# Row sums of absolute values: one Abs pass in place of two Relu passes, and the last tile fetched in five pieces

## Chip, cores, metric

One core of a Trainium2 chip. The time is the device time of one execution in microseconds; it lies about 1.8 us above the span of the profile, which is the window of the instructions in the trace.

DVE is VectorE, ACT is ScalarE, SPq is the sequencer of SyncE, which issues the DMAs, POOL is GpSimd. A semaphore is a counter by which one unit tells another that it is done. A "landing" is the moment at which a DMA's semaphore lets a waiting instruction go. A load is moved in packets, here one for each row, shared out over 16 DMA engines; each engine adds a small one of 4 bytes at the end of its part. So a load of 128 whole rows is 9 packets an engine: the profile before counts 1296 packets for its nine DMAs, 9 x 9 x 16.

## The reference

```python
batch, dim = 1024, 4096                     # x: float32
def reference(x, axis):                     # axis = -1
    return np.sum(np.abs(x), axis=axis).astype(np.float32)
```

16.8 MB are read, 4 KB are written, and there is next to no arithmetic: the input must come in, and nothing more.

## The kernel before

Partition p holds the rows 8p to 8p+7; tile t is the t-th of these rows in all partitions, 128 x 4096. All eight tiles have a buffer of their own, so all loads are issued at once. VectorE reduces 2560 columns of each tile with a built-in absolute value. ScalarE takes the other 1536 twice, as Relu(x) and Relu(-x), each with a running sum.

```python
d_act = (int(D * 0.6 / (0.96 + 0.6)) // 128) * 128      # 1536
d_dve = D - d_act                                        # 2560
for t in range(T):                                       # T = 8
    xt = xs.tile([P, D], f32, name="xt")
    nc.sync.dma_start(out=xt, in_=x_t[t])
    nc.vector.tensor_reduce(out=dve_acc[:, t : t + 1], in_=xt[:, :d_dve],
        axis=mybir.AxisListType.X, op=mybir.AluOpType.add, apply_absolute_value=True)
    nc.scalar.activation(out=scratch, in_=xt[:, d_dve:], func=Relu, scale=1.0,
        accum_out=pos_acc[:, t : t + 1])                 # (names shortened)
    nc.scalar.activation(out=scratch, in_=xt[:, d_dve:], func=Relu, scale=-1.0,
        accum_out=neg_acc[:, t : t + 1])
nc.vector.tensor_add(out=pos_acc, in0=pos_acc, in1=neg_acc)
nc.vector.tensor_add(out=dve_acc, in0=dve_acc, in1=pos_acc)
nc.sync.dma_start(out=out_pt, in_=dve_acc)
```

## Time and profile before

| | before |
|---|---|
| time, median of 16 runs | 49.93 us (49.83 to 50.10) |
| span of the profiled run | 48.1 us |
| first tile lands | 7.87 us |
| tile to tile | 4.89 us |
| last tile lands | 42.1 us |
| result issued | 45.80 us |
| from there to the end of the span | 2.26 us |

The lower rows are read from the timeline: the start of a VectorE reduce that waited for its load is the landing, give or take 0.02 us. Read them as a budget: what comes before the last landing is transfer, and what comes after it is tail. The loads themselves, in the profile's list of DMA issues (size of each, and median time from issue to landing):

```profile
xt<-in_x_dram SPq DMA_DIRECT2D x8, 2048.0 KB, 22.6
out_dram<-dve_acc SPq DMA_DIRECT2D x1, 4.0 KB, 1.4
```

Eight loads of 2 MB stand in one queue, so a load "takes" 22.6 us, nearly all of it waiting behind others. The small one of the result shows the bare latency, 1.4 us.

### The profile page before, as it was taken

To read this page: it belongs to the slowest core of one execution; us is meant where nothing else is said; L and a number is where in the kernel's file an instruction comes from. 1 tells how busy PE (TensorE), PEld (TensorE's weight loads), DVE (VectorE), ACT (ScalarE), POOL (GpSimd) and SP (SyncE) were. 2 spreads that over 40 slices of the span, in tenths; PEclk is the share of its full clock that TensorE was granted. 3 is DMA by queue.
4 is the path that set the end of the run, shared out by engine and by line. 5 is a ranking of instruction groups with operands and counts; after the bars stand their busy time and mean duration, and the time that the engine had idled before them with its cause. 6 is when DMAs were issued, how large, how long until landed. Compare 5 with 4: busy or idle time off the path is not lost.

```text
span 48.1 us, 106 instructions
## 1 busy us (share of the span) xinstructions
DVE 22.9 (48%) x10; ACT 26.5 (55%) x33; POOL 0.2 (0%) x4
## 2 busy tenths in 40 slices
DVE  0000004980399039902991199109920993099500
ACT  3600004991399329931994199509960996089700
POOL 1000000000000000000000000000000000000000
DMA  0969999999999999999999999999999899300000
GB/s 0 218 286 409 409 436 436 436 423 436 436 436 436 436 436 436 436 436 436 436 436 436 436 436 436 436 409 423 423 423 436 382 436 423 136 0 0 0 3 0
DMA packets 1296, 16.78 MB, mean 349 GB/s; under 512 B 272, under 2 KB 272, under 8 KB 272
## 3 DMA queue, kind: packets, MB, share of 16 engines
q1 hardware_dynamic: 1296, 16.78, 83.1%
HBM read 16.78 MB, written 0.00 MB: 349 GB/s over the span
## 4 chain that ended last, share of the span: by engine, by line
DMA 79%; SPq 7%; ACT 6%; issue 1%; DVE 1%; ACTq 0%
DMA xt<-in_x_dram 79%; SPq L45 7%; ACT scratch L55 3%; ACT scratch L62 3%; DVE pos_acc L71 0%; DVE dve_acc L72 0%; ACTq L104 0%; ACTq L55 0%
## 5 line engine op out<-in xcount | busy, mean ns | idle before, releaser
L47 DVE TENSOR_REDUCE dve_acc<-xt 128x1 f32<-128x2560 f32 x8 | 22.6, 2820 | 22.4 <-DMA xt<-in_x_dram 22.4
L55 ACT ACTIVATE scratch<-xt 128x1536 f32<-128x1536 f32 x8 | 11.9, 1483 | 17.9 <-DMA xt<-in_x_dram 17.9
L62 ACT ACTIVATE scratch<-xt 128x1536 f32<-128x1536 f32 x8 | 11.9, 1483 | 0.2
L55 ACT ACT_TABLE_LOAD x1 | 1.3, 1283 | 0.7 <-PEq L90 0.7
L62 ACT ACTIVATION_READ_ACCUMULATOR scratch<-xt 128x1 f32 x8 | 1.5, 186 | 0.0
L55 ACT ACTIVATION_READ_ACCUMULATOR scratch<-xt 128x1 f32 x8 | 1.5, 186 | 0.0
L71 DVE TENSOR_TENSOR pos_acc<-pos_acc,neg_acc 128x8 f32<-128x8 f32 x1 | 0.2, 168 | 0.5 <-ACT scratch L62 0.5
L72 DVE TENSOR_TENSOR dve_acc<-dve_acc,pos_acc 128x8 f32<-128x8 f32 x1 | 0.2, 169 | 0.0
L90 POOL MEMSET const-bfloat16-1.0<- 128x1 bf16 x1 | 0.1, 103 | 0.0
L90 POOL MEMSET const-uint8-127<- 128x1 uint8 x1 | 0.1, 103 | 0.0
L90 POOL MEMSET const-float32-1.0<- 128x1 f32 x1 | 0.1, 100 | 0.0
L90 POOL MEMSET const-float32-0.0<- 128x1 f32 x1 | 0.1, 99 | 0.2 <-issue 0.2
## 6 DMA issues: line engine op xcount, KB each, us to landing
xt<-in_x_dram SPq DMA_DIRECT2D x8, 2048.0 KB, 22.6
out_dram<-dve_acc SPq DMA_DIRECT2D x1, 4.0 KB, 1.4
```

The lines of the kernel that those rows point to most:

```text
L45: nc.sync.dma_start(out=xt, in_=x_t[t])
L47: nc.vector.tensor_reduce(out=dve_acc[:, t : t + 1], in_=xt[:, :d_dve], axis=mybir.AxisListType.X, op=mybir.AluOpType.add, apply_absolute_ ...
L55: nc.scalar.activation(out=scratch, in_=xt[:, d_dve:], func=mybir.ActivationFunctionType.Relu, scale=1.0, accum_out=pos_acc[:, t : t + 1],)
L62: nc.scalar.activation(out=scratch, in_=xt[:, d_dve:], func=mybir.ActivationFunctionType.Relu, scale=-1.0, accum_out=neg_acc[:, t : t + 1],)
L71: nc.vector.tensor_add(out=pos_acc, in0=pos_acc, in1=neg_acc)
L72: nc.vector.tensor_add(out=dve_acc, in0=dve_acc, in1=pos_acc)
L90: nc = _bacc.Bacc("TRN2", target_bir_lowering=False, num_devices=1)
```

## The change

The intent: shorten the work that is left when the last data has landed. ScalarE does one Abs pass in place of two Relu passes; the whole tiles are split 2048 to 2048; the last tile comes in five loads, each given to one engine; one reduce over a common accumulator (zeroed by GpSimd at the start) replaces the two adds. The diff, cut to its core (an unused option for TensorE, off in the file, is left out):

```diff
+LAST = ((1280, 1), (1280, 0), (768, 1), (384, 0), (384, 1))  # columns, 1 for VectorE
+    acc = small.tile([P, T, S], f32, name="acc")             # S = 5
+    nc.gpsimd.memset(acc, 0.0)
     for t in range(T):
-        xt = xs.tile([P, D], f32, name="xt")
-        nc.sync.dma_start(out=xt, in_=x_t[t])
-        nc.vector.tensor_reduce(... in_=xt[:, :d_dve] ...)
-        nc.scalar.activation(... func=Relu, scale=1.0 ...)
-        nc.scalar.activation(... func=Relu, scale=-1.0 ...)
+        if t < T - 1:
+            xw = whole.tile([P, D], f32, name="xw")
+            nc.sync.dma_start(out=xw, in_=x_t[t])
+            nc.vector.tensor_reduce(out=acc[:, t, 2:3], in_=xw[:, :2048], ...)
+            nc.scalar.activation(out=scratch, in_=xw[:, 2048:], func=Abs, accum_out=acc[:, t, 0:1])
+            continue
+        for lo, hi, eng in chunks:                           # the five pieces of LAST
+            xt = xs.tile([P, max_chunk], f32, name="xt")[:, :cols]
+            nc.sync.dma_start(out=xt, in_=x_t[t][:, lo:hi])
+            if eng == 0:
+                nc.scalar.activation(... in_=xt, func=Abs, accum_out=acc[:, t, si : si + 1])
+            else:
+                nc.vector.tensor_reduce(out=acc[:, t, si : si + 1], in_=xt, ...)
-        nc.vector.tensor_add(out=pos_acc, in0=pos_acc, in1=neg_acc)
-        nc.vector.tensor_add(out=dve_acc, in0=dve_acc, in1=pos_acc)
-    nc.sync.dma_start(out=out_pt, in_=dve_acc)
+    nc.vector.tensor_reduce(out=out_sb, in_=acc, axis=X, op=add)
+    nc.sync.dma_start(out=out_pt, in_=out_sb)
```

More of the change, by code (lines that the diff above doesn't have):

```diff
@@ L7 @@
 from concourse._compat import with_exitstack
+LAST = ((1280, 1), (1280, 0), (768, 1), (384, 0), (384, 1))
+PE_WARM = False
+LOAD_BUFS = 5
 @with_exitstack
@@ L26 @@
     f32 = mybir.dt.float32
-    d_act = (int(D * 0.6 / (0.96 + 0.6)) // 128) * 128
-    d_dve = D - d_act
+    chunks = []
+    lo = 0
+    for c, eng in LAST:
+        chunks.append((lo, lo + c, eng))
+        lo += c
+    assert lo == D
+    S = len(LAST)
     x_t = x.rearrange("(p t) d -> t p d", t=T)
     out_pt = out.rearrange("(p t) -> p t", t=T)
-    xs = ctx.enter_context(tc.tile_pool(name="xs", bufs=min(T, 8)))
-    acc = ctx.enter_context(tc.tile_pool(name="acc", bufs=1))
+    xs = ctx.enter_context(tc.tile_pool(name="xs", bufs=LOAD_BUFS))
+    whole = ctx.enter_context(tc.tile_pool(name="whole", bufs=T - 1))
     small = ctx.enter_context(tc.tile_pool(name="small", bufs=1))
-    dve_acc = acc.tile([P, T], f32, name="dve_acc")
-    pos_acc = acc.tile([P, T], f32, name="pos_acc")
-    neg_acc = acc.tile([P, T], f32, name="neg_acc")
-    scratch = small.tile([P, d_act], f32, name="scratch") if d_act else None
-    for t in range(T):
-        xt = xs.tile([P, D], f32, name="xt")
-        nc.sync.dma_start(out=xt, in_=x_t[t])
-        nc.vector.tensor_reduce(
-            out=dve_acc[:, t : t + 1],
-            in_=xt[:, :d_dve],
-            axis=mybir.AxisListType.X,
-            op=mybir.AluOpType.add,
-            apply_absolute_value=True,
-        )
-        if d_act:
-            nc.scalar.activation(
-                out=scratch,
-                in_=xt[:, d_dve:],
-                func=mybir.ActivationFunctionType.Relu,
-                scale=1.0,
-                accum_out=pos_acc[:, t : t + 1],
+    if PE_WARM:
+        psum = ctx.enter_context(tc.tile_pool(name="psum", bufs=2, space=bass.MemoryType.PSUM))
+        ones = small.tile([P, 1], f32, name="ones")
+        nc.vector.memset(ones, 1.0)
+    acc = small.tile([P, T, S], f32, name="acc")
+    scratch = small.tile([P, 2048], f32, name="scratch")
+    out_sb = small.tile([P, T], f32, name="out_sb")
+    nc.gpsimd.memset(acc, 0.0)
+    max_chunk = max(hi - lo for lo, hi, _ in chunks)
+    for t in range(T):
+        if t < T - 1:
+            xw = whole.tile([P, D], f32, name="xw")
+            nc.sync.dma_start(out=xw, in_=x_t[t])
+            nc.vector.tensor_reduce(
+                out=acc[:, t, 2:3],
+                in_=xw[:, :2048],
+                axis=mybir.AxisListType.X,
+                op=mybir.AluOpType.add,
+                apply_absolute_value=True,
             )
@@ L63 @@
                 out=scratch,
-                in_=xt[:, d_dve:],
-                func=mybir.ActivationFunctionType.Relu,
-                scale=-1.0,
-                accum_out=neg_acc[:, t : t + 1],
-            )
-    if d_act:
-        nc.vector.tensor_add(out=pos_acc, in0=pos_acc, in1=neg_acc)
-        nc.vector.tensor_add(out=dve_acc, in0=dve_acc, in1=pos_acc)
-    nc.sync.dma_start(out=out_pt, in_=dve_acc)
+                in_=xw[:, 2048:],
+                func=mybir.ActivationFunctionType.Abs,
+                accum_out=acc[:, t, 0:1],
+            )
+            continue
+        si = 0
+        for lo, hi, eng in chunks:
+            cols = hi - lo
+            xt = xs.tile([P, max_chunk], f32, name="xt")[:, :cols]
+            nc.sync.dma_start(out=xt, in_=x_t[t][:, lo:hi])
+            if eng == 0:
+                nc.scalar.activation(
+                    out=scratch[:, :cols],
+                    in_=xt,
+                    func=mybir.ActivationFunctionType.Abs,
+                    accum_out=acc[:, t, si : si + 1],
+                )
+                si += 1
+            else:
+                nc.vector.tensor_reduce(
+                    out=acc[:, t, si : si + 1],
+                    in_=xt,
+                    axis=mybir.AxisListType.X,
+                    op=mybir.AluOpType.add,
+                    apply_absolute_value=True,
+                )
+                si += 1
+                if PE_WARM:
+                    pe_out = psum.tile([1, 256], f32, name="pe_out")
+                    nc.tensor.matmul(
+                        pe_out, lhsT=ones, rhs=xt[:, :256], start=True, stop=True
+                    )
+        assert si == S
+    nc.vector.tensor_reduce(
+        out=out_sb, in_=acc, axis=mybir.AxisListType.X, op=mybir.AluOpType.add
+    )
+    if PE_WARM:
+        pe_out2 = psum.tile([T, T], f32, name="pe_out2")
+        nc.tensor.matmul(pe_out2, lhsT=out_sb, rhs=out_sb, start=True, stop=True)
+    nc.sync.dma_start(out=out_pt, in_=out_sb)
 _INS = ['x', 'axis']
```

## The prediction

> **What bounds the kernel now.** I read the page first: the 40 slices (part 2) with the chain that ended last (part 4), to see whether transfers or engines fill the middle; then the groups (part 5) for durations; then the timeline of the last microseconds, because a kernel that is bound by transfers can only be shortened at its two ends.
>
> ```profile
> DVE  0000004980399039902991199109920993099500
> ACT  3600004991399329931994199509960996089700
> DMA  0969999999999999999999999999999899300000
> GB/s 0 218 286 409 409 436 436 436 423 436 436 436 436 436 436 436 436 436 436 436 436 436 436 436 436 436 409 423 423 423 436 382 436 423 136 0 0 0 3 0
> ...
> DMA 79%; SPq 7%; ACT 6%; issue 1%; DVE 1%; ACTq 0%
> ```
>
> Each slice is 1.2 us. The transfers are full from the fourth slice to the 34th, and both engines fall idle once in every tile. 79% of the final chain is the load of x. After the 35th slice nothing is moved, but the engines work for three more slices and the result is written: that is the tail that can be shortened.
>
> ```profile
> L47 DVE TENSOR_REDUCE dve_acc<-xt 128x1 f32<-128x2560 f32 x8 | 22.6, 2820 | 22.4 <-DMA xt<-in_x_dram 22.4
> L55 ACT ACTIVATE scratch<-xt 128x1536 f32<-128x1536 f32 x8 | 11.9, 1483 | 17.9 <-DMA xt<-in_x_dram 17.9
> L62 ACT ACTIVATE scratch<-xt 128x1536 f32<-128x1536 f32 x8 | 11.9, 1483 | 0.2
> L55 ACT ACT_TABLE_LOAD x1 | 1.3, 1283 | 0.7 <-PEq L90 0.7
> L55 ACT ACTIVATION_READ_ACCUMULATOR scratch<-xt 128x1 f32 x8 | 1.5, 186 | 0.0
> L71 DVE TENSOR_TENSOR pos_acc<-pos_acc,neg_acc 128x8 f32<-128x8 f32 x1 | 0.2, 168 | 0.5 <-ACT scratch L62 0.5
> ```
>
> Both engines idle only for the load. The timeline, in which a row starts with its start and its length in us:
>
> ```profile
> 37.23 2.82 DVE L47 TENSOR_REDUCE dve_acc<-xt 128x1 f32<-128x2560 f32 x1 [2.07 <-DMA xt<-in_x_dram]
> ...
> 42.12 2.82 DVE L47 TENSOR_REDUCE dve_acc<-xt 128x1 f32<-128x2560 f32 x1 [2.07 <-DMA xt<-in_x_dram]
> 42.18 1.48 ACT L55 ACTIVATE scratch<-xt 128x1536 f32<-128x1536 f32 x1 [1.71 <-DMA xt<-in_x_dram]
> 43.57 0.19 ACT L55 ACTIVATION_READ_ACCUMULATOR scratch<-xt 128x1 f32 x1
> 43.79 1.48 ACT L62 ACTIVATE scratch<-xt 128x1536 f32<-128x1536 f32 x1
> 45.18 0.19 ACT L62 ACTIVATION_READ_ACCUMULATOR scratch<-xt 128x1 f32 x1
> 45.40 0.17 DVE L71 TENSOR_TENSOR pos_acc<-pos_acc,neg_acc 128x8 f32<-128x8 f32 x1 [0.46 <-ACT scratch L62]
> 45.60 0.17 DVE L72 TENSOR_TENSOR dve_acc<-dve_acc,pos_acc 128x8 f32<-128x8 f32 x1
> 45.80 0.35 SPq L73 DMA_DIRECT2D out_dram<-dve_acc  x1
> ```
>
> Tiles land 42.12 - 37.23 = 4.89 us apart (the other tiles the same, from 7.87 us on). In a tile DVE works 2.82 us and ACT about 3.2, so DVE waits 2.07 and ACT 1.71: the middle is bound by transfer alone. The last tile lands at about 42.10, and the result's DMA is issued at 45.80. These 3.7 us are one tile on ScalarE (two Relu passes, 3.2 us) and two small adds. From the issue to the end of the span, 48.1, are 2.3 us, and the timed 50.0 us are 1.9 above the span; the change touches neither.
>
> **What the Trainium skill says.** (1) "ScalarE: Activation LUTs", What ACT_TABLE_LOAD costs: an ACTIVATE with immediate scale and bias takes 186 ns + 0.833 ns per element, and a table load 1283 ns. At 1536 elements that is 1466 ns; the trace has 1483, and 1283 for the load, so it agrees. Its section Table sets says abs and relu are in every set, so no second load; the order of instructions of the changed kernel has one load too. (2) "VectorE: DVE Perf Modes", the perf-mode tier table: tensor_reduce runs in 1x mode alone. The errata section of the page has (N+151)/0.96 ns for an fp32 tensor_tensor; used for the reduce, an estimate, it gives 2824 ns at N = 2560, against 2820 in the trace, so I use it for all reduces. (3) "DMA: Bandwidth & Descriptors", Bandwidth: its rule is 1 MiB or more a DMA, and Why small descriptors are slow gives some 3 cycles of fixed cost a packet. The trace has only 16 KB rows and the 32-byte result, so it doesn't show rows of 1.5 to 5 KB. (4) "Perfetto Trace Analysis", DMA Optimizations: splitting DMAs may let work start sooner; that is the change's intent, and the trace before, unsplit, cannot show it.
>
> **The change part by part.**
>
> *First seven tiles: two Relu passes become one Abs pass, split 2048 to 2048.* ACT per tile: 203 + 0.833 x 2048 = 1.91 us (203 is what the measured 1483 leaves), and with the accumulator's read about 2.1, from 3.2. DVE: (2048+151)/0.96 = 2.29 us, from 2.82. Worth nothing: both end before the next tile, which comes 4.89 us later.
>
> *Table load.* In the new order the load waits for the first tile, as the first activation waits for GpSimd's memset besides. So ACT begins tile 0 at 7.87 + 1.28 + 0.1 = 9.25 and is done at about 11.35. Tile 1 lands at 12.75. Hidden, with 1.4 us to spare.
>
> *Issues.* The queue now has 12 loads; the last four wait for landings of tiles 0 to 3 in turn (at 7.9, 12.8, 17.6 and 22.5 us by the starts above). Their data is due only from 38.8 us, so no gap. The result's DMA waits for tile 4's landing besides, 27.4 us: long over.
>
> *Last tile in five pieces.* A tile of 4096 columns takes 4.89 us, so 1.194 ns a column. From tile 6 at 37.23:
> piece 0 (1280, DVE) lands at 38.76; piece 1 (1280, ACT) at 40.29; piece 2 (768, DVE) at 41.20; piece 3 (384, ACT) at 41.66; piece 4 (384, DVE) at 42.12, if the rows' size costs nothing.
> DVE: tile 6 until 37.23 + 2.29 = 39.52; piece 0 (1431/0.96 = 1.49) until 41.03; piece 2 (0.96) from 41.22 to 42.18; piece 4 (535/0.96 = 0.56) from 42.20 to 42.76.
> ACT: tile 6 until 39.4; piece 1 (203 + 1066 = 1.27, with the read 1.4) from 40.35 until 41.75; piece 3 (203 + 320 = 0.52, with the read 0.62) from 41.80 to 42.4. So ACT is done before DVE.
> Final reduce over 40 elements: (40+151)/0.96 = 0.20 us, from 42.79 to 42.99; the result is issued at about 43.02, against 45.80.
> The tail after the landing falls from 3.70 to about 0.90: 2.8 us saved. It takes the place of the two adds too (0.37 with their gap).
>
> *What the pieces cost the transfer.* Each of the 16 DMA engines gets 8 rows and a completion a piece: 45 packets in place of 9 for the last tile, 36 more. Per packet: the skill's 3 cycles would be some 3 to 4 ns at the 850 MHz that the page names for the fabric, 0.13 us in all (an estimate). An upper bound from the trace: in its packet records the result's 144 packets, 9 an engine, pass in 0.19 us, 21 ns each; 36 x 21 = 0.76 us if all that came on top. I take 0.2 us.
>
> Sum: 50.0 - 2.8 + 0.2 = 47.4; the DVE reduce of piece 2 ends close to piece 4's landing, and a landing later by 0.2 hides a little of DVE's wait, 0.05. Predicted 47.3 us (span about 45.4).
>
> **The rivals.**
> A. The small rows slow the transfer by more than I allow. For: the skill's rule of 1 MiB, and rows of 1.5 KB are a tenth of those measured. Against: there is no gap between today's loads (4.89 us a tile is 429 GB/s, against 436 in the best slices), the pieces queue behind one another on full engines, and they are an eighth of the data. At the upper bound 47.9; to undo the gain the last tile's 4.89 us would have to become 7.7.
> B. An engine becomes the end: DVE behind on its three pieces, or false waits between DVE and ACT, which now write one accumulator tile. For: DVE's slack at piece 2 is just 0.19 us. Against: in the order of instructions each piece waits only for its own DMA and its own engine. If DVE were 0.5 us late: 47.8.
> C. The gain is hidden, because the kernel is bound by transfers (79% of the chain), and halving ACT's work helps an engine that waits anyway: 50.0. True for seven tiles, but the tail lies after the last transfer, so nothing hides it.
> D. The late issues leave a bubble or the late table load delays a tile: each would cost up to 1 us. The slacks above (16 us and 1.4 us) speak against it.
>
> **Range and chances.** With no cost of the pieces it is 47.15; with A's bound or B 47.8 to 47.9. The runs before spread by 0.2. So 46.9 to 47.9. Faster by over 2% means below 49.0, which needs 1.7 us of surprise: 0.96 faster, 0.03 same, 0.01 slower.
>
> **What would show it.** In the profile after: tiles 0 to 6 land within 0.1 us of before; ACT's first activation begins near 9.25; DVE's last piece begins at 42.2 to 42.5 and takes 0.56; the final reduce waits for DVE and not ACT; the result is issued at about 43.2; and the tail from there is 2.3 us still. It is wrong if the last piece lands after 42.9 (A), if DVE starts the last piece well after its landing or waits for ACT (B), if the slices before the end show a dip in GB/s (D), or if the span falls and the timed runs don't.

## The result, and the profile after

| | before | after |
|---|---|---|
| time, median | 49.93 us (16 runs) | 47.59 us (10 runs, 47.48 to 48.13) |
| ratio | | 0.954 (0.952 to 0.956) |
| tile 6 lands | 37.23 us | 37.23 us |
| last landing | 42.1 us | 42.37 us |
| result issued | 45.80 us | 43.28 us |
| from there to the end | 2.26 us | 2.43 us |

A ratio is the mean time of one kernel's fast runs over that of the other's of the same rounds, so not quite the ratio of the medians quoted. The kernel was run once more among the experiments: 47.69 us, ratio 0.952.

The same views as before. First the slices of the page for the transfers (each now 1.14 us), and the shares of the final chain:

```profile
DMA  0969999899999999999999999999999799995000
GB/s 0 215 244 459 444 430 445 373 401 430 459 459 459 444 416 401 387 416 459 459 459 444 430 387 387 430 444 459 459 430 430 323 408 417 392 395 188 0 4 0
...
DMA 88%; SPq 3%; DVE 2%; issue 1%; DVEq 0%
```

The transfer's share of the chain is 88%, up from 79%. Only part of that is the shorter span: the 37.9 us of transfer in the chain before would be 83% of 45.7 us. The rest is the way in which the chain is followed: it enters the transfers at 2.10 us in place of 4.17, because the load of the last piece was issued only when tile 3 had landed. The swings of GB/s look worrying and mean little, as a slice holds only some 30 packets of 16 KB (430 GB/s for 1.14 us); the landings are sharper, and all seven whole tiles land within 0.1 us of before. The groups:

```profile
L61 DVE TENSOR_REDUCE acc<-xw 128x1 f32<-128x2048 f32 x7 | 16.0, 2286 | 23.5 <-DMA xw<-in_x_dram 23.5
L68 ACT ACTIVATE scratch<-xw 128x2048 f32<-128x2048 f32 x7 | 13.4, 1909 | 16.1 <-DMA xw<-in_x_dram 16.0
L68 ACT ACT_TABLE_LOAD x1 | 1.3, 1283 | 7.9 <-DMA xw<-in_x_dram 7.9
L105 DVE TENSOR_REDUCE out_sb<-acc 128x8 f32<-128x40 f32 x1 | 0.2, 195 | 0.1
```

Each engine works less per tile and waits more for loads. The table load waited 7.9 us for the first tile, as the order of instructions said. The timeline of the end (start, length, what):

```profile
37.23 2.29 DVE L61 TENSOR_REDUCE acc<-xw 128x1 f32<-128x2048 f32 x1 [2.61 <-DMA xw<-in_x_dram]
...
39.44 1.48 DVE L90 TENSOR_REDUCE acc<-xt 128x1 f32<-128x1280 f32 x1
40.47 1.27 ACT L82 ACTIVATE scratch<-xt 128x1280 f32<-128x1280 f32 x1 [1.18 <-DMA xt<-in_x_dram]
41.40 1.54 DVE L90 TENSOR_REDUCE acc<-xt 128x1 f32<-128x768 f32 x2 [0.49 <-DMA xt<-in_x_dram]
...
41.98 0.52 ACT L82 ACTIVATE scratch<-xt 128x384 f32<-128x384 f32 x1
42.41 0.19 ACT L82 ACTIVATION_READ_ACCUMULATOR scratch<-xt 128x1 f32 x1
43.06 0.20 DVE L105 TENSOR_REDUCE out_sb<-acc 128x8 f32<-128x40 f32 x1
43.28 0.35 SPq L111 DMA_DIRECT2D out_dram<-out_sb  x1
```

(The row of 41.40 merges two reduces, of 768 and of 384 columns.) And the last steps of the chain that ended last (start, length, what):

```profile
22.55 19.82 DMA xt<-in_x_dram
...
42.40 0.56 DVE acc L90
...
43.06 0.20 DVE out_sb L105
```

So the final chain is: last piece lands at 42.37, 0.56 us reduce, 0.10 us until the final reduce may start, 0.20 us, issue. After the last landing 0.9 us pass in place of 3.7. From that gain, 2.8, two things are lost again: the last landing is 0.27 us later, and the time from the result's issue to the end is 0.17 us longer.

### The profile page after: what moved, and what is told of

Same layout as the page of the kernel before. It is cut to its first block, busy times and chain, and to the rows that moved or that the text cites. A ratio compares the mean times of both kernels' runs of the same rounds, so it can differ in the third digit from the quotient of the medians.

```text
span 45.7 us, 102 instructions
## 1 busy us (share of the span) xinstructions
DVE 19.1 (42%) x11; ACT 17.3 (38%) x19; POOL 0.3 (1%) x5
## 4 chain that ended last, share of the span: by engine, by line
DMA 88%; SPq 3%; DVE 2%; issue 1%; DVEq 0%
DMA xw<-in_x_dram 45%; DMA xt<-in_x_dram 43%; SPq L60 3%; DVE acc L90 1%; DVE out_sb L105 0%; DVEq L105 0%
## 5 line engine op out<-in xcount | busy, mean ns | idle before, releaser
L61 DVE TENSOR_REDUCE acc<-xw 128x1 f32<-128x2048 f32 x7 | 16.0, 2286 | 23.5 <-DMA xw<-in_x_dram 23.5
L68 ACT ACTIVATE scratch<-xw 128x2048 f32<-128x2048 f32 x7 | 13.4, 1909 | 16.1 <-DMA xw<-in_x_dram 16.0
L90 DVE TENSOR_REDUCE acc<-xt 128x1 f32<-128x1280 f32 (+2 forms) x3 | 3.0, 994 | 0.5 <-DMA xt<-in_x_dram 0.5
L82 ACT ACTIVATE scratch<-xt 128x1280 f32<-128x1280 f32 (+1 forms) x2 | 1.8, 896 | 1.3 <-DMA xt<-in_x_dram 1.2
L68 ACT ACTIVATION_READ_ACCUMULATOR scratch<-xw 128x1 f32 x7 | 1.3, 186 | 0.0
L82 ACT ACTIVATION_READ_ACCUMULATOR scratch<-xt 128x1 f32 x2 | 0.4, 186 | 0.0
```

The lines of the kernel that those rows point to most:

```text
L61: nc.vector.tensor_reduce(out=acc[:, t, 2:3], in_=xw[:, :2048], axis=mybir.AxisListType.X, op=mybir.AluOpType.add, apply_absolute_value=True,)
L68: nc.scalar.activation(out=scratch, in_=xw[:, 2048:], func=mybir.ActivationFunctionType.Abs, accum_out=acc[:, t, 0:1],)
L82: nc.scalar.activation(out=scratch[:, :cols], in_=xt, func=mybir.ActivationFunctionType.Abs, accum_out=acc[:, t, si : si + 1],)
L90: nc.vector.tensor_reduce(out=acc[:, t, si : si + 1], in_=xt, axis=mybir.AxisListType.X, op=mybir.AluOpType.add, apply_absolute_value=True,)
```

## The experiments

All eleven runs give the reference's result. Kernels shared a chip with runs of the kernel before. Ratios are against that kernel, in the same rounds.

### One Abs pass alone, all tiles whole

```diff
 # the kernel before, with
-    d_act = (int(D * 0.6 / (0.96 + 0.6)) // 128) * 128
-    d_dve = D - d_act
+    d_dve = 2048
-  two activations with func=Relu, scale=1.0 and -1.0
+  one activation with func=Abs, accum_out=acc2[:, t, 0:1]
-  two tensor_add
+  one tensor_reduce over acc2
```

> The kernel before with one Abs pass and a 2048 to 2048 split, all eight tiles whole. Theory 1 (the tail after the last landing is what falls, and each part of the change shortens it): DVE ends 2.29 us after the last start at 42.12, the final reduce takes about 0.2, so the result is issued at about 44.7 instead of 45.80, and the time is 49.93 - 1.1 = 48.8 us. Rival (only the cut of the last tile pays; the one pass helps an engine that waits anyway): 49.9.

Measured: 48.80 us, ratio 0.979 (0.977 to 0.981). The end of its timeline:

```profile
42.25 2.29 DVE L45 TENSOR_REDUCE acc<-xt 128x1 f32<-128x2048 f32 x1 [2.60 <-DMA xt<-in_x_dram]
44.65 0.17 DVE L59 TENSOR_REDUCE out_sb<-acc 128x8 f32<-128x16 f32 x1
44.85 0.35 SPq L62 DMA_DIRECT2D out_dram<-out_sb  x1
```

Theory 1 holds, the rival falls. The lighter work is worth nothing in seven tiles, but the eighth lies behind the last landing, and there it is worth 1.1 us. This kernel changes three things at once: the one pass, the even split and the single final reduce. The last is about 0.1 of the 1.1 (from the end of the last engine to the issue 0.31 us, before 0.43); the pass and the split were not separated.

### The cut alone, with two Relu passes

```diff
 # the changed kernel, with
-                in_=xw[:, :2048]            # VectorE
+                in_=xw[:, :2560]
-  one activation with func=Abs, for whole tiles and for pieces
+  two activations with func=Relu, scale=1.0 and -1.0, each with a sum of its own (S = 7)
```

> The changed kernel with two Relu passes put back (whole tiles 2560 to 1536 as before, the five pieces kept, each ScalarE piece twice). Theory 1: ScalarE gets behind: tile 6 until 40.4, piece 1 twice until 43.3, piece 3 twice until 44.6, so the result is issued at about 44.9 and the time is about 49.2 us: the cut alone gives only some 0.7 of the 2.3, and the two parts together more than the sum of each alone. Rival (the cut alone pays): 47.6 to 47.9.

Measured: 49.16 us, ratio 0.986 (0.985 to 0.988). Its timeline:

```profile
40.66 1.27 ACT L91 ACTIVATE scratch<-xt 128x1280 f32<-128x1280 f32 x1
42.06 1.27 ACT L91 ACTIVATE scratch<-xt 128x1280 f32<-128x1280 f32 x1
...
44.10 0.52 ACT L91 ACTIVATE scratch<-xt 128x384 f32<-128x384 f32 x1
44.74 0.21 DVE L115 TENSOR_REDUCE out_sb<-acc 128x8 f32<-128x56 f32 x1 [1.66 <-ACT scratch L91]
```

No row of ScalarE here shows a wait for a load: with two passes it falls behind, and VectorE waits 1.66 us for it at the end. Theory 1 holds. The two parts need one another: alone they give 1.07 (49.87 - 48.80) and 0.71 us (49.87 - 49.16), together 2.34 (49.93 - 47.59), although the single final reduce is in both and so is counted twice in the sum of the two. The cut pays something even where ScalarE falls behind, but in full only where the engines keep up with the pieces.

### What the pieces cost the transfer: packets or DMAs

The packet records of the trace after give the median time of one row by its size: 611 ns for 16384 bytes, 200 for 5120, 125 for 3072, 65 for 1536. A line through these is about 8.5 ns plus bytes/27.2. Two kernels test whether the cost belongs to the packet or to the DMA; both give each engine as many columns as the kernel before, though not the same ones.

```diff
 # the kernel before, 4 KB blocks in the same eight DMAs
-        xt = xs.tile([P, D], f32, name="xt")
-        nc.sync.dma_start(out=xt, in_=x_t[t])
+        xt = xs.tile([P, 4, D // 4 + 16], f32, name="xt")
+        nc.sync.dma_start(out=xt[:, :, : D // 4], in_=x_t[t].rearrange("p (b c) -> p b c", b=4))
```

> The kernel before with the same eight loads, but each row of 16 KB written as four blocks of 4 KB with a gap between, so four times the packets in the same number of DMAs. Theory 1 (a packet has a fixed cost of some 8.5 ns, read from 611 ns at 16384 bytes, 200 at 5120, 125 at 3072 and 65 at 1536): 24 more packets an engine and tile x 8 tiles x 8.5 ns = 1.6 us more: about 51.5 us. Rival (what the pieces cost is a cost of each DMA, its completion, and not of each packet): 49.9.

```diff
 # as above, each block a DMA of its own, 32 in all
+        for b in range(4):
+            nc.sync.dma_start(out=xt[:, b, : D // 4],
+                              in_=x_t[t][:, b * (D // 4) : (b + 1) * (D // 4)])
```

> As the run with 4 KB blocks, but each block is a DMA of its own: 32 loads in place of 8 with the same packets. Theory 1: only 24 more completions of 9 ns an engine, 0.2 us more than the run with 4 KB blocks: about 51.8 us. Rival (each DMA costs some 0.065 us, the 0.26 us of the four added pieces divided by four): 24 x 0.065 = 1.6 us more than the run with 4 KB blocks.

Measured: 51.18 us (ratio 1.026, 1.024 to 1.028) and 51.77 us (1.038, 1.036 to 1.040). Landings of two tiles in the middle of each, first with eight DMAs, then with 32:

```profile
13.27 2.82 DVE L49 TENSOR_REDUCE dve_acc<-xt 128x1 f32<-128x2560 f32 x1 [2.22 <-DMA xt<-in_x_dram]
18.30 2.82 DVE L49 TENSOR_REDUCE dve_acc<-xt 128x1 f32<-128x2560 f32 x1 [2.21 <-DMA xt<-in_x_dram]
```

```profile
13.81 2.82 DVE L51 TENSOR_REDUCE dve_acc<-xt 128x1 f32<-128x2560 f32 x1 [2.24 <-DMA xt<-in_x_dram]
18.86 2.82 DVE L51 TENSOR_REDUCE dve_acc<-xt 128x1 f32<-128x2560 f32 x1 [2.23 <-DMA xt<-in_x_dram]
```

Packets cost: a tile takes 5.04 us (mean of the seven intervals of the first kernel) in place of 4.89, so 0.15 us for 24 more packets an engine, 6 ns each; I had expected 8.5 ns, and 1.6 us in place of the 1.3 measured. DMAs as such cost next to nothing in a full queue: with four times as many the interval is 5.05. The rival, 0.065 us for each DMA, would have made it 5.24. Still, the second kernel is 0.59 us slower than the first, three times what I had expected. About half of that lies outside the trace: all six runs of the second kernel took 2.1 us more than their spans, all other kernels 1.7 to 1.8; why is open. The median spans differ by 0.25 us (49.65 and 49.4). The profile of the second kernel is of one of its two slowest executions (52.08 us, span 50.0); in it the difference comes with the first tile, which lands at 8.75 in place of 8.23 us. The last window before that (window, length, busy of DVE, ACT, POOL, clock, DMA share, GB/s), eight DMAs and then 32:

```profile
4.80:8.00 3.20, 0.00 (x0) 0.00 (x0) 0.00 (x0) 1.00 1.03 421
```

```profile
4.80:8.00 3.20, 0.00 (x0) 0.00 (x0) 0.00 (x0) 1.00 1.00 379
```

In this window the engines are as busy but move a tenth less. In the two windows before it they had moved more, though (56 against 38 GB/s up to 2.40 us, 384 against 358 from there to 4.80), so by 8.00 us both kernels had moved about 2.3 MB, more than the 2.1 MB of the first tile. What differs is how far apart the 16 DMA engines are: a load has landed when the last of them has reported, and by the trace's landing records the 16 reports of a load in mid-run lie within about 0.33 us in the first kernel and 0.85 in the second. Why they drift apart there is left open. In the changed kernel, whose small loads come last, the 16 reports of the last piece lie within 0.25 us.

### The table load ahead of the loop

```diff
     nc.gpsimd.memset(acc, 0.0)
+    nc.scalar.activation(out=scratch[:, :1], in_=acc[:, 0, 0:1], func=Abs)
```

> The changed kernel with one activation on one element ahead of the loop, so that the table load runs at the start and no longer waits for the first tile. Theory 1 (the late table load is hidden in the slack of tile 0): the same as the changed kernel within 0.1 us, 47.6. Rival (the late load costs part of its 1.28 us): 47.1 or less.

Measured: 47.55 us, ratio 0.951 (0.949 to 0.953); the changed kernel's own ratios are 0.954 and 0.952. The load of the table did move to the start, and ScalarE began tile 0 at its landing:

```profile
0.73 1.28 ACT L55 ACT_TABLE_LOAD   x1 [0.73 <-PEq L133]
7.94 1.91 ACT L73 ACTIVATE scratch<-xw 128x2048 f32<-128x2048 f32 x1 [5.71 <-DMA xw<-in_x_dram]
```

The time did not follow beyond the runs' scatter: the late table load was hidden.

### Eight loads, so that the result has the first semaphore again

The prediction did not foresee the 0.17 us at the end. The trace's records of the SP queue after the issue of the result show them (us from that issue, worked out from the trace's instruction records):

```
before:  wait 1, wait 2, wait 3 pass; wait 4 (result) passes at 1.43; wait 5; end at 2.26
after:   wait 1 passes; wait 2 (result) passes at 1.43; waits 3, 4, 5 of 0.06 each; end at 2.43
```

Before its end the program waits for every semaphore in a fixed order. The loads take eight semaphores in turn. With eight loads the result gets the first one, which is late in the list; with twelve it gets the fifth, which is early, and three further waits that could have passed meanwhile are gone through after it.

```diff
 # the changed kernel: seven whole tiles in three loads of 4, 2 and 1 tiles
+GROUPS = {0: 4, 4: 2, 6: 1}  # first tile of a load: tiles in it
+                g = whole.tile([P, n, D + 16], f32, name=f"g{t}")   # gap: rows stay 16 KB
+                nc.sync.dma_start(out=g[:, :, :D], in_=x.rearrange("(p t) d -> p t d", t=T)[:, t : t + n, :])
```

> The changed kernel with the seven whole tiles fetched by three loads (4, 2 and 1 tiles, rows still 16 KB each, gaps between the tiles' groups only), so eight loads in all, as before, and no load waits for another's landing; the result's DMA then has the first semaphore again, which the wait list at the end comes to last. Theory 1 (the 0.17 us by which the time from the result's issue to the end grew, 2.26 to 2.43, comes from three waits of 61 ns that are gone through only after the result's landing): from issue to end 2.26 again or a little less, and the time 0.1 to 0.2 lower than the changed kernel, about 47.4. Rival (the growth is noise, or comes from the result's DMA itself): 47.6, with 2.4 from issue to end.

Measured: 47.55 us, ratio 0.951 (0.948 to 0.953). The profile has the result issued at 43.43 and a span of 45.71, so 2.28 us from issue to end, close to the 2.26 that were expected. Yet the time did not fall against its neighbour in the same rounds, 47.55 too: tile 6 landed at 37.41 in place of 37.23, which ate the gain. I had no reason to expect that; the next section comes back to it.

```diff
 # the same with rows of 32 KB: two tiles that lie side by side in memory
+ROWS = {0: 2, 4: 2}          # tiles in one row of a load
```

> As the run with eight loads, but the first six tiles are fetched in rows of 32 KB (two tiles that lie side by side in memory). Theory 1 (fixed cost of 8.5 ns a packet): 24 packets an engine fewer, 0.2 us lower than the run with eight loads, about 47.2. Rival (a packet over some size is no cheaper, or is split): same as the run with eight loads.

Measured: 47.45 us, ratio 0.948 (0.946 to 0.950), 0.1 us below the kernel with 16 KB rows, with overlapping intervals. The packet records agree with the line through the sizes: 1213 ns for 32768 bytes, where 8.5 + 32768/27.2 gives 1213. But the profiled run shows no gain in the landings (tile 6 at 37.45). Not clear by itself.

### Three pieces, each shared by both engines

The durations that the profiles gave were enough to choose pieces by a small calculation of landings and engine times. It gives 43.3 us for the result's issue in the changed kernel (measured 43.28), and its best form with three pieces was tried, with the changed kernel itself beside it.

> The changed kernel itself, unaltered, so that the three runs beside it are compared with it on the same chip in the same rounds. Both theories: 47.6 us, 43.3 from the start to the result's issue and 2.43 from there to the end.

```diff
-LAST = ((1280, 1), (1280, 0), (768, 1), (384, 0), (384, 1))
+LAST = ((1088, 1280), (576, 544), (352, 256))  # columns for VectorE, for ScalarE
+            nc.vector.tensor_reduce(... in_=xt[:, :eng] ...)      # eng: VectorE's columns
+            nc.scalar.activation(... in_=xt[:, eng:], func=Abs ...)
```

> The last tile in three pieces (2368, 1120 and 608 columns), each shared by both engines, in place of five that belong to one engine each. Sum by the durations measured so far (DVE (N+151)/0.96 ns, ACT 203 + 0.833 N and 0.13 for its read, 8.5 ns a packet and 4 bytes/27.2 ns a column and row): the last landing 0.16 us earlier for 16 packets fewer, the result issued at about 43.13 in place of 43.3, so 47.4 us. Rival (the tail is set by the last landing and fixed costs alone, the form of the pieces is indifferent): 47.6.

```diff
+GROUPS = {0: 1, 1: 2, 3: 2, 5: 1, 6: 1}   # eight loads, rows of 16 KB
```

> As the run with three shared pieces, with tiles 1 and 2, and 3 and 4, fetched by one load each, rows of 16 KB: eight loads, the first of one tile. Theory 1: the wait list at the end takes 2.28 us from the result's issue in place of 2.43, and the 0.15 us by which the landings came later in the run with eight loads came from its first load of four tiles, so they don't come later here: about 47.25 us. Rival (any larger load spreads the 16 engines and gives the gain back): 47.4.

```diff
+ROWS = {1: 2, 3: 2}                       # the double loads with rows of 32 KB
```

> As the run with three shared pieces and eight loads, but the two double loads with rows of 32 KB: 16 packets an engine fewer, 0.14 us at 8.5 ns each: about 47.1 us. Rival (larger packets spread the engines and give it back): the same as the run with eight loads.

| | time | ratio to before (95%) | tile 6 lands | result issued | issue to end |
|---|---|---|---|---|---|
| the changed kernel again | 47.69 | 0.952 (0.949 to 0.955) | 37.21 | 43.25 | 2.43 |
| three shared pieces | 47.37 | 0.947 (0.944 to 0.949) | 37.43 | 43.30 | 2.44 |
| and eight loads | 47.20 | 0.942 (0.939 to 0.945) | 37.30 | 43.15 | 2.28 |
| and rows of 32 KB | 47.06 | 0.940 (0.938 to 0.943) | 37.20 | 43.08 | 2.28 |

The times came out within 0.1 us of what was expected, in the order expected; the issue with three shared pieces did not (43.30, expected 43.13), as tile 6 landed later. Two readings are well founded. With eight loads the part from issue to end is 2.28 us in each of four profiles (the two here and the two of the section before), against 2.43 and 2.44 with twelve or ten loads. Over all thirteen profiles it is 2.20 to 2.28 with eight loads or 32, and 2.42 to 2.44 with ten or twelve: with 32 the result has the first of the eight semaphores again, so the result's place counts, and not the number of loads as such. And the tail from tile 6's landing to the result's issue is 5.87 us with three shared pieces (43.30 - 37.43), against 6.04 (43.25 - 37.21) with five; over all profiles with one Abs pass 5.85 to 5.88 with three and 6.02 to 6.05 with five. The tail of the last kernel:

```profile
40.08 2.63 DVE L93 TENSOR_REDUCE acc<-xt 128x1 f32<-128x1088 f32 x3 [0.58 <-DMA xt<-in_x_dram]
42.31 0.42 ACT L100 ACTIVATE scratch<-xt 128x256 f32<-128x256 f32 x1
42.85 0.20 DVE L109 TENSOR_REDUCE out_sb<-acc 128x8 f32<-128x48 f32 x1
43.08 0.35 SPq L115 DMA_DIRECT2D out_dram<-out_sb  x1
```

The 32 KB rows are a further 0.14 us in the medians, as counted, but neighbouring intervals overlap.

Partly open is when tile 6 lands. It differs by 0.2 us between profiles, also between kernels whose loads up to there are the same (37.21 above, 37.39 in the kernel with the cut alone). By the landing records the 16 engines are apart again: the first of them reports at 36.88 and the last at 37.19 in the changed kernel run again, at 36.88 and 37.41 with three shared pieces. Profiles also catch different executions: that of the changed kernel run again is its fastest (47.46 us, median 47.69), that of three shared pieces its slowest (47.52, median 47.37), so their landings should not be compared closely. For the late landing in the first kernel with eight loads the packet records speak for its large first load: by 4.80 us that kernel and the one with rows of 32 KB beside it had moved 0.89 MB, the kernels with a first load of one tile in rows of 16 KB 0.96 to 1.01, and 0.1 MB takes 0.2 us at 430 GB/s (an estimate). With one profile each that is not shown.

The last kernel beats both others: 6.0% below the kernel before, and 1.2% below the changed one (0.940/0.952).

## Why the prediction was right

47.3 us were predicted, in a range of 46.9 to 47.9; 47.59 were measured. Its steps one by one:

- *The middle is bound by the transfer, and only the tail can be shortened.* Right. Tile 6 landed at 37.23 in both traces, although both engines had less to do. With all tiles whole, the lighter work paid 1.1 us, what it took from the last tile. ("Both engines idle only for the load" is not quite what the lines show: VectorE also waits 0.5 us for ScalarE, in the tail.)
- *Durations.* Right to within 20 ns: reduces of 2286 ns at 2048 columns (2.29 predicted) and 0.55 at 384 (0.56), an activation of 1909 (1.91), a final reduce of 195 (0.20).
- *Tail of 3.7 us to 0.9.* Right: 43.28 - 42.37 = 0.91. A little luck is in it: VectorE started the last piece 0.03 us after its landing and not 0.08 as in the schedule without cost, and the final reduce started 0.10 us after the last piece and not 0.03.
- *VectorE and not ScalarE ends last.* Right: ScalarE's last read ended at 42.60, VectorE's last piece at 42.96.
- *Table load and late issues are hidden.* Right. Moving the table load changed nothing beyond scatter, and the landings show no bubble. The dip in GB/s that was named as a sign of D is in the view (323 in the slice from 35.4 to 36.6 us), but tile 6, the next to land, is not late: 37.23 in both traces.
- *The pieces cost the transfer 0.2 us, at most 0.76.* Right in kind, a little small in size: the last piece landed at 42.37 in place of 42.10, 0.27 us. The 36 more packets at the 8.5 ns that the packet records give make 0.31. Taking 0.05 off again because a late landing "hides a little of DVE's wait" was borne out: the last reduce started at 42.40, 0.20 after the 42.20 of the schedule without cost, while the landing was 0.25 after that schedule's 42.12. (The 47.15 given for no cost takes this 0.05 off too, where it doesn't apply; by the same sum it is 47.2.)
- *The change touches neither the 2.3 us after the issue nor the 1.9 above the span.* Wrong for the first: 2.43 in place of 2.26, by the order of the waits at the end of the program, which depends on which semaphore the result gets.

Small terms make up the difference. By the prediction's own steps the result is issued at 43.02 + 0.20 - 0.05 = 43.17 us, and with the 2.26 of before the span is 45.43. Measured were 43.28 and 45.71, so 0.28 more: 0.05 for the later start of the last reduce, 0.07 for the later final reduce, 0.17 at the end, to rounding. From the span to the time two errors of 0.1 cancel: the prediction added 1.9, the profiled execution shows 1.8 (47.49 us), and the median of the runs lies 0.1 above that execution. That the sum of the time comes out so close is in part luck.

Of the rivals, A (costlier small rows) is real but stays at 0.27 us. B (an engine becomes the end) did not happen, if narrowly: VectorE ended the piece before at 42.36, just 0.01 us before the last landing. The kernel with two Relu passes shows what B looks like. C (the gain is hidden) holds for seven tiles and not for the eighth. D did not occur.

## What to carry to other kernels

In a kernel that is bound by its input, find the last landing and count what is left behind it: that, and not the busy shares, is what can be saved by lighter compute. A cut of the last load pays in full only where the engines keep pace with the pieces; check it piece by piece with the measured fixed time of each instruction, as a cut and a lighter pass can be worth more together than the sum of each. When a few tenths of a microsecond matter, look also behind the last instruction of the kernel: the number of loads changed how many waits were left there after the result had landed.

## What the Trainium skill lacked or had wrong

- "DMA: Bandwidth & Descriptors", Why small descriptors are slow, gives some 3 cycles for a packet, which would be 3.5 ns at the 850 MHz that the page names for the fabric (an estimate). Here a packet cost more: 611 ns for 16384 bytes and 65 for 1536 leave about 8.5 ns beside the bytes, and by the landings 24 more packets cost 0.15 us, 6 ns each. The page's own measured 10.5 ns for a packet of its smallest transfer, under Bandwidth, lies nearer.
- The same page, Bandwidth, advises loads of 1 MiB or more. In a full queue the size of a DMA did not matter: tiles in loads of 2 MB and of 0.5 MB with the same packets came 5.04 and 5.05 us apart. The size of a row did. (The kernel with the small loads was 0.59 us slower in all; about half of that lies outside the trace, and the cause is open.)
- "VectorE: DVE Perf Modes" gives no duration for tensor_reduce. Its (N+151)/0.96 ns for tensor_tensor fits it: 2286 ns at 2048 columns (2291 by the formula), 553 at 384 (557), 195 at 40 (199).
- "ScalarE: Activation LUTs" mentions the accumulator output but not its read, a separate instruction of 186 ns after every activation that sums.
- No page that I read has the wait list at the end of a program: after the result has landed, each further wait in it costs about 0.06 us, and how many there are depends on which semaphore the result has (2.20 to 2.44 us from issue to end).
